# One matmul operand of 512 columns for both parts of the tokens in the first tiles of u, with the selection cut into smaller steps

## The chip, the cores and the metric

The kernel runs on one core of one Trainium2 chip. The metric is the device time of the whole program in microseconds, the median of several runs.

## What is computed

A trunk of two layers over 256 tokens of width 1024. Each layer has a mixer (Mamba-2 SSD in the first, retention in the second), a PEER expert network and a gated per-layer input. The change lies in the expert network, which is dense here: every expert's inner product with every token is computed, and a sparse gate picks from them.

```python
def peer_ffn(h, w_q, sub_keys, u, v):
    q = (xt @ w_q).reshape(T, PEER_HEADS, 2, PEER_HALF)
    sc = jnp.einsum('thcd,hckd->thck', q, sub_keys)
    s1, i1 = lax.top_k(sc[:, :, 0], K)
    s2, i2 = lax.top_k(sc[:, :, 1], K)
    cand = (s1[..., :, None] + s2[..., None, :]).reshape(T, PEER_HEADS, K * K)
    cand_idx = (i1[..., :, None] * NK + i2[..., None, :]).reshape(T, PEER_HEADS, K * K)
    top_s, top_pos = lax.top_k(cand, K)
    idx = jnp.take_along_axis(cand_idx, top_pos, axis=-1)
    gate = jax.nn.softmax(top_s, axis=-1)
    ...
        hid = jax.nn.gelu(jnp.einsum('tkd,td->tk', u[ib], xb), approximate=False)
        return jnp.einsum('tk,tkd->td', (gb * hid), v[ib])
```

There are 256 tokens (T), 8 heads, 128 keys, 16 picks per head (K) and 16384 experts; u and v are 16384 x 1024 in float32.

## The kernel before

Products in float32 are made from numbers split into a high and a low part in fp32r: wh and wl of a weight tile, xh and xl of the tokens. A product is wh xh + wh xl + wl xh.

The function `peer` has, in each layer, a u stage of 128 tiles (128 experts each) and a v stage of 128 tiles. For a u tile, `u_maker` issues four loads of 128 KB on SP and, as soon as they have landed, a transpose of 32 x 32 blocks on DVE (L514); then ACT casts the tile to wh (L519) and POOL subtracts to wl (L522). `get` (called once per tile) starts the cast and the subtraction of the next tile and the load and transpose of the tile after that. Tiles up to 55 are loaded into four places of the arena (`UEND`); from tile 56 on loads and transposes share the four buffers `raw`. wh and wl have two buffers each. The sum of a tile gathers in one of two PSUM banks named `m`: 16 matmuls of 256 columns with wh, alternating xh and xl (L1241, L1242), then 8 with wl (L1245). ACT takes the Gelu from there into H (L1205), one tile later.

Beside these tiles DVE works on the selection: the top 16 of both halves' scores (`sel_codes`), sums of pairs (`sel_sums`), their top 16 (`sel_cand`), positions (`sel_pos`), the softmax (`sel_gate`, whose Exp is on ACT, `sel_sum`, `sel_split`, `sel_ratio`) and the look-up of the picked keys (`sel_idx`: compare, multiply and add over 1024 elements). These steps stand in a list `bg` with a cost each. After a tile's `get`, `pump(1700)` takes steps from the list until the credit is used up. The list ends with `sel_tr`, which transposes the results on TensorE (L1107).

When the list is empty, the gates follow: `g_slot` runs once per tile and moves 64 batches of four tokens through one-hot rows on DVE (`g_hot`), scaling on ACT (`g_lo`), eight small matmuls into a bank `g` (`g_mm`, L1185) and the product with H (`g_apply`, L1199 on DVE). Then the v stage multiplies H, split by `wsplit` (L1256), with v: 12 matmuls of 512 columns per tile (L1279).

All engines run their instructions in the order in which the code records them, in one queue for each engine; waits between engines are semaphores. In the names below arena is the big buffer (H, scores and all of the selection), raw the load buffers, ps the accumulators' banks.

Of the kernel before, what the change touches and what calls it, by code (L numbers as in the profile page):

```python
# [8 lines left out]
F32 = mybir.dt.float32  # L9
# [79 lines left out]
def trunk(ctx: ExitStack, tc: tile.TileContext, a, out, dbg=None, stop=None):  # L89
# [862 lines left out]
    def peer(l, st):  # L952
# [14 lines left out]
        e1 = A[:, S0 + 9856:S0 + 10368].bitcast(F16).rearrange("p (a b c) -> p a b c", a=4, b=16)  # L967
# [71 lines left out]
        def sel_cand(tb, h):  # L1039
            u = 128 * tb + 16 * h  # L1040
            top([cand[:, tb, h + i] for i in range(2)], cand2, [ts_[:, tb, h + i] for i in range(2)],
                [pu[:, u + 16 * i:u + 16 * i + 16] for i in range(2)])
# [23 lines left out]
        def sel_idx(tb, h, c, part):  # L1066
            u = slice(128 * tb + 16 * h, 128 * tb + 16 * h + 64)
            if part == 0:
                dve.tensor_tensor(e1, io16.unsqueeze(1).unsqueeze(1).to_broadcast([P, 4, 16, 16]),
                                  pa[:, c, u].rearrange("p (a b) -> p a b", a=4).unsqueeze(3).to_broadcast(  # L1070
                                      [P, 4, 16, 16]), op=OP.is_equal)
            if part == 1:
                s4 = si.rearrange("p (t h c k) -> p t h c k", t=2, h=8, c=2)[:, tb, h:h + 4, c]
                dve.tensor_mul(e1, e1, s4.unsqueeze(2).to_broadcast([P, 4, 16, 16]))
            if part == 2:
                dve.tensor_reduce(sel[:, c, u].rearrange("p (a b) -> p a b", a=4), e1, axis=AX.X, op=OP.add)
# [38 lines left out]
        bg = [(3100, sel_codes, tb, c0 + c) for c0 in (0, 8) for tb in range(2) for c in range(0, 8, 2)]  # L1115
# [6 lines left out]
        for i in range(4):  # L1122
            bg += [(600, sel_ratio, i), idx[8 + i]]
# [343 lines left out]
```

## Time and profile before

| | us |
|---|---|
| median of 3 runs | 2187.97 (2187.0 to 2191.56) |
| profiled execution | 2188.43 |
| its span, first to last instruction | 2186.7 |
| TensorE busy | 2125.1 (97%) |
| DVE busy | 1577.8 (72%) |
| ACT busy | 1208.1 (55%) |
| POOL busy | 828.5 (38%) |

Busy shares are means over stages with different limits. Within a u stage the start times of TensorE's tiles tell the pace; a wait that ends last shows as idle time before an instruction, with its releaser. The u stage of the first layer runs from 312.3 to 722.4 us after the span's start, that of the second from 1373.9 to 1786.3.

### The profile page before, as it was taken

How to read it: one execution, taken by the hardware profiler on the slowest of the kernel's cores; microseconds unless marked ns; L12 is line 12 of the kernel's file. 1: busy time of each engine (PE TensorE's matmuls, PEld its weight loads, DVE VectorE, ACT ScalarE, POOL GpSimd, SP SyncE). 2: the span in 40 equal slices, each digit the busy share in tenths (PEclk: the TensorE clock that was granted, in tenths of full speed). 3: DMA queues.
4: the chain of work that ended last, by engine and by line, in shares of the span. 5: the costliest groups of instructions: out<-in, count | busy, mean ns of one | idle time of the engine just before them, and what ended most of it. 6: DMA issues, size and time to landing. Idle time of an engine off the chain costs nothing. (4 is left out here: it accounts for less than half of the span.)

```text
span 2186.7 us, 39792 instructions
## 1 busy us (share of the span) xinstructions
PE 2125.1 (97%) x15013; PEld 1967.9 (90%) x15013; DVE 1577.8 (72%) x2641; ACT 1208.1 (55%) x2077; POOL 828.5 (38%) x384
## 2 busy tenths in 40 slices
PE   8988999999999999999999999999999999999997
PEld 8978899999999888888898999999999998888886
DVE  7777578888999655555687466989799985555556
ACT  5654444547888544444554444545588874444444
POOL 3243268877777100000033223888777740000001
PEclk9999999999999999999999999999999999999999
DMA  5423477645555666556556456765555555555553
GB/s 185 145 78 97 161 198 194 184 133 165 155 156 154 188 195 194 193 193 193 188 179 187 128 169 182 192 184 152 153 150 158 155 170 193 195 194 194 194 189 107
DMA packets 219577, 370.27 MB, mean 169 GB/s; under 512 B 24240, under 2 KB 163192, under 8 KB 219384
## 3 DMA queue, kind: packets, MB, share of 16 engines
q1 hardware_dynamic: 219064, 367.19, 56.5%
q8 instruction: 118, 1.93, 0.4%
q14 instruction: 75, 0.61, 0.1%
q10 hardware_dynamic: 320, 0.53, 0.1%
HBM read 364.48 MB, written 1.05 MB: 167 GB/s over the span
## 5 line engine op out<-in xcount | busy, mean ns | idle before, releaser
L139 DVE TENSOR_TENSOR wl<-raw,wh 128x1024 fp32r<-128x1024 f32 x379 | 468.0, 1238 | 402.0 <-ACT wh L136 401.7
L136 ACT CAST wh<-raw 128x1024 fp32r<-128x1024 f32 x429 | 450.6, 1052 | 501.0 <-PE ps L1279 359.0
L522 POOL TENSOR_TENSOR wl<-raw,wh 128x1024 fp32r<-128x1024 f32 x256 | 618.5, 2417 | 200.8 <-ACT wh L519 192.1
L1241 PE MATMUL m<-X,wh 128*128 128x256 f32 x2048 | 514.0, 289 | 0.6 <-ACT arena L1205 0.5
L1279 PE MATMUL ps<-wh,X 128*128 128x512 f32 x2048 | 507.3, 389 | 1.9 <-ACT X L1256 1.9
L1242 PE MATMUL m<-X,wh 128*128 128x256 f32 x2048 | 502.9, 283 | 0.0
L1279 PEld LDWEIGHTS ps<-wh,X 128*128 128x128 f32 x2048 | 384.1, 188 | 82.0 <-ACT X L1256 2.3
L519 ACT CAST wh<-raw 128x1024 fp32r<-128x1024 f32 x256 | 269.0, 1051 | 264.7 <-issue 150.1
L1241 PEld LDWEIGHTS m<-X,wh 128*128 128x128 f32 x2048 | 392.7, 192 | 1.2 <-ACT arena L1205 1.0
L1242 PEld LDWEIGHTS m<-X,wh 128*128 128x128 f32 x2048 | 393.6, 192 | 0.0
L199 PE MATMUL ps<-X,wh 128*128 128x256 f32 x2368 | 331.6, 290 | 12.4 <-ACT wh L136 8.0
L341 POOL TENSOR_TENSOR arena<-arena 128x512 f32<-128x512 f32 x15 | 22.6, 1504 | 815.8 <-ACT arena L339 807.8
L199 PEld LDWEIGHTS ps<-X,wh 128*128 128x128 f32 x2368 | 304.8, 196 | 18.3 <-ACT wh L136 10.2
L1245 PE MATMUL m<-X,wl 128*128 128x256 f32 x2048 | 288.0, 283 | 0.1
L1279 PE MATMUL ps<-wl,X 128*128 128x512 f32 x1024 | 274.7, 389 | 0.0
L1245 PEld LDWEIGHTS m<-X,wl 128*128 128x128 f32 x2048 | 264.8, 192 | 1.1 <-POOL wl L522 1.1
L1279 PEld LDWEIGHTS ps<-wl,X 128*128 128x128 f32 x1024 | 192.2, 188 | 40.0
L514 DVE STREAM_TRANSPOSE raw<-raw 128x1024 f32<-128x1024 f32 x144 | 179.0, 1243 | 39.8 <-DMA raw<-in_peer_u 33.2
L139 POOL TENSOR_TENSOR wl<-raw,wh 128x1024 fp32r<-128x1024 f32 x50 | 124.7, 2500 | 180.3 <-ACT wh L136 149.2
L199 PE MATMUL ps<-X,wl 128*128 128x256 f32 x1184 | 177.3, 287 | 14.2 <-DVE wl L139 10.3
L199 PEld LDWEIGHTS ps<-X,wl 128*128 128x128 f32 x1184 | 157.5, 194 | 17.5 <-DVE wl L139 12.2
L1179 ACT ACTIVATE ol<-ol,G 128x128 f16<-128x128 f16 x512 | 162.8, 398 | 0.1
(263 smaller groups left out, 2015.5 us busy)
## 6 DMA issues: line engine op xcount, KB each, us to landing
raw<-in_peer_v SPq DMA_DIRECT2D x256, 512.0 KB, 4.3
raw<-in_peer_u SPq DMA_DIRECT2D x576, 128.0 KB, 3.0
arena<-in_peer_u SPq DMA_DIRECT2D x448, 128.0 KB, 3.3
raw<-in_ret_w_in SPq DMA_DIRECT2D x48, 512.0 KB, 3.9
raw<-in_ssd_w_in SPq DMA_DIRECT2D x41, 512.0 KB, 3.8
raw<-in_peer_w_q SPq DMA_DIRECT2D x32, 512.0 KB, 4.7
raw<-in_ssd_w_out SPq DMA_DIRECT2D x16, 512.0 KB, 3.8
raw<-in_ple_gate SPq DMA_DIRECT2D x16, 512.0 KB, 4.3
```

The source lines that it names most:

```text
L136: act.copy(wh[:, :n], r[:, :n])
L139: (eng or dve).tensor_sub(wl[:, :n], r[:, :n], wh[:, :n].bitcast(F32))
L199: pe.matmul(self.t[n // 2][:, n % 2], w[:, n * P:(n + 1) * P], x, start=st, stop=sp_, skip_group_check=True)
L341: pool.tensor_add(self.sq[:, 0], self.sq[:, 0], self.sq[:, b])
L514: dve.transpose(t.rearrange("p (k b i) -> p b k i", k=8, b=4), r.rearrange("p (b k i) -> p b k i", k=8, b=4))
L519: act.copy(wh, t)
L522: pool.tensor_sub(wl, t, wh.bitcast(F32))
L1179: act.activation(hl[:, 1, j], hl[:, 0, j], AF.Copy, scale=G1[:, t:t + 1])
L1241: pe.matmul(last, wh[:, s], xh, start=k == 0, stop=False)
L1242: pe.matmul(last, wh[:, s], xl, start=False, stop=False)
L1245: pe.matmul(last, wl[:, s], xh, start=False, stop=k == KD - 1)
L1279: pe.matmul(sums[b], h[:, tb * P:(tb + 1) * P], w[:, n * 512:(n + 1) * 512], start=i == 0 and p == 0, stop=i == P - 1 and p == 2)
```

## The change

While selection steps remain, a u tile is wide: xh and xl of a chunk, which lie in one buffer, are given as one moving operand of 512 columns, so the bank's first half gathers wh xh (+ wl xh) and its second half wh xl. ACT copies the second half into H, DVE adds the first half to it, and ACT takes the Gelu in place one tile later. Copy and add are recorded ahead of the next tile's `get`. The selection's steps are cut: each `top` step is one of its five parts. `sel_idx` is made new: for each of 16 ranks one operation compares and multiplies at once into 16-bit numbers, and `sel_add` adds over the ranks. The list is 107400 credits long instead of 114900.

```diff
-        def sel_idx(tb, h, c, part):
-            u = slice(128 * tb + 16 * h, 128 * tb + 16 * h + 64)
-            if part == 0:
-                dve.tensor_tensor(e1, io16.unsqueeze(1).unsqueeze(1).to_broadcast([P, 4, 16, 16]),
...
-            if part == 2:
-                dve.tensor_reduce(sel[:, c, u].rearrange("p (a b) -> p a b", a=4), e1, axis=AX.X, op=OP.add)
+        def sel_idx(c, r0):
+            v = pa[:, c].rearrange("p (h k) -> p h k", k=16)
+            for r in range(r0, r0 + 4):
+                k = slice(r if c else r // 8 * 8, 16)
+                n = 16 - k.start
+                s1 = si.rearrange("p (h c k) -> p h c k", c=2, k=16)[:, :, c, r:r + 1]
+                dve.scalar_tensor_tensor(e1[:, r, :, k], v[:, :, k], float(r), s1.to_broadcast([P, 16, n]),
+                                         op0=OP.is_equal, op1=OP.mult)
+
+        def sel_add(c, i):
+            dve.tensor_reduce(sel[:, c].rearrange("p (h k) -> p h k", k=16)[:, :, 8 * i:8 * i + 8],
+                              e1[:, :8 * i + 8, :, 8 * i:8 * i + 8].rearrange("p r h k -> p h k r"), axis=AX.X, op=OP.add)
...
-        bg = [(3100, sel_codes, tb, c0 + c) for c0 in (0, 8) for tb in range(2) for c in range(0, 8, 2)]
+        bg = [(620, sel_codes, tb, c0 + c, i) for c0 in (0, 8) for tb in range(2) for c in range(0, 8, 2)
+              for i in range(5)]
         for tb in range(2):
             bg += [(1800, sel_sums, tb)]
-            bg += [(2500, sel_cand, tb, h) for h in range(0, 8, 2)]
+            bg += [(500, sel_cand, tb, h, i) for h in range(0, 8, 2) for i in range(5)]
...
-        idx = [(1200, sel_idx, tb, h, c, k) for tb in range(2) for h in (0, 4) for c in range(2) for k in range(3)]
+        idx = []
+        for c, cost in ((0, (1900, 1900, 1200, 1200)), (1, (1900, 1500, 1000, 700))):
+            idx += [(n, sel_idx, c, 4 * i) for i, n in enumerate(cost)] + [(1800, sel_add, c, 0), (3200, sel_add, c, 1)]
...
             if k in (4, 6):
+                both = X[:, xn[0] % 3]
                 xh, xl = split_x(xm[:, 2 * k - 8:2 * k - 4])
-                xp.extend((xh[:, i], xl[:, i]) for i in range(4))
+                xp.extend((xh[:, i], xl[:, i], both[:, :, i]) for i in range(4))
...
-        last, since = None, 0
+        last, since, wide, late = None, 0, False, None
         for i in range(P):
+            if late is not None:
+                act.activation(H[:, late], H[:, late], AF.Gelu)
+                late = None
+            if wide:
+                act.copy(H[:, i - 1], last[:, T:])
+                dve.tensor_add(H[:, i - 1], last[:, :T], H[:, i - 1])
+                late = i - 1
             wh, wl = get()
             if last is not None:
-                g_slot(i, gelu(i - 1, last))
+                g_slot(i, gelu(i - 1, last) if not wide else lambda: None)
...
+            wide = bool(bg)
+            for k, (xh, xl, xx) in enumerate(xp):
                 s = slice(k * P, (k + 1) * P)
-                pe.matmul(last, wh[:, s], xh, start=k == 0, stop=False)
-                pe.matmul(last, wh[:, s], xl, start=False, stop=False)
-            for k, (xh, xl) in enumerate(xp):
+                if wide:
+                    pe.matmul(last, wh[:, s], xx, start=k == 0, stop=k == KD - 1, skip_group_check=True)
...
+            for k, (xh, xl, xx) in enumerate(xp):
                 s = slice(k * P, (k + 1) * P)
-                pe.matmul(last, wl[:, s], xh, start=False, stop=k == KD - 1)
+                pe.matmul(last[:, :T], wl[:, s], xh, start=False, stop=k == KD - 1, skip_group_check=wide)
```

In the built program 56 tiles of each layer are wide (tiles 0 to 55). SP's and POOL's instructions keep their order. What moves on ACT and DVE shows at three places.

ACT at the start of the u stage, the kernel before: the cast for tile 1, two copies of scores (L1001), the cast for tile 2, the first Gelu (L1205) with its table load, and the next copies.

```order
L519 CAST wh<-raw 128x1024 [waits DVE_49,PE_49,Pool_49] x2
L1001 COPY arena<-g 128x512 [waits PE_49] x2
L519 CAST wh<-raw 128x1024 [waits DVE_49,Pool_49]
L1205 ACT_TABLE_LOAD
L1205 ACTIVATE arena<-m 128x256
L1001 COPY arena<-g 128x512 [waits PE_49] x2
L519 CAST wh<-raw 128x1024 [waits DVE_49,Pool_49]
```

The same place now; L1239 is the copy of a tile's second half, L1236 the Gelu in place.

```order
L519 CAST wh<-raw 128x1024 [waits DVE_49,PE_49,Pool_49] x2
L1001 COPY arena<-g 128x512 [waits PE_49] x2
L1239 COPY arena<-m 128x256
L519 CAST wh<-raw 128x1024 [waits DVE_49,Pool_49]
L1001 COPY arena<-g 128x512 [waits PE_49] x2
L1236 ACT_TABLE_LOAD
L1236 ACTIVATE arena<-arena 128x256 [waits DVE_49]
L1239 COPY arena<-m 128x256
L519 CAST wh<-raw 128x1024 [waits DVE_49,Pool_49]
```

The table load and the first Gelu stood ahead of the second pair of score copies and stand behind it now, and a copy stands ahead of each cast.

ACT around the Exp of the softmax (L1084 of the kernel before), before:

```order
L1205 ACTIVATE arena<-m 128x256 [waits PE_49]
L519 CAST wh<-raw 128x1024 [waits DVE_49,PE_49,Pool_49]
L1205 ACTIVATE arena<-m 128x256 [waits PE_49]
L1084 ACT_TABLE_LOAD
L1084 ACTIVATE arena<-arena 128x256 [waits DVE_49]
L519 CAST wh<-raw 128x1024 [waits PE_49,Pool_49]
L1205 ACT_TABLE_LOAD
L1205 ACTIVATE arena<-m 128x256 [waits PE_49]
```

The same place now (L1086 is the Exp):

```order
L1239 COPY arena<-m 128x256 [waits PE_49]
L519 CAST wh<-raw 128x1024 [waits DVE_49,Pool_49]
L1086 ACT_TABLE_LOAD
L1086 ACTIVATE arena<-arena 128x256 [waits DVE_49]
L1236 ACT_TABLE_LOAD
L1236 ACTIVATE arena<-arena 128x256
L1239 COPY arena<-m 128x256 [waits PE_49]
L519 CAST wh<-raw 128x1024 [waits Pool_49]
```

The cast after the Exp stood directly behind it; now the second table load, a Gelu and a copy stand between them. Each copy waits for TensorE, and the cast behind it no longer does.

DVE in the middle of the codes, before: whole pairs of five steps between transposes.

```order
L1009 MAX arena<-arena 128x8 x2
L1011 MAX_INDEX arena<-arena 128x8 [waits DVE_49] x2
L1014 MATCH_REPLACE arena<-arena 128x128 x2
L1009 MAX arena<-arena 128x8 [waits DVE_49] x2
L1011 MAX_INDEX arena<-arena 128x8 [waits DVE_49] x2
L514 STREAM_TRANSPOSE raw<-arena 128x4x8x32 [waits DMAHW2_49,DMAHW1_49,DMAHW7_49,DMAHW0_49,Pool_49]
L514 STREAM_TRANSPOSE raw<-arena 128x4x8x32 [waits DMAHW5_49,DMAHW4_49,DMAHW6_49,DMAHW3_49,Pool_49]
```

The same place now, with the add of a tile's halves at L1240:

```order
L1240 TENSOR_TENSOR arena<-m,arena 128x256 [waits Activation_49]
L514 STREAM_TRANSPOSE raw<-arena 128x4x8x32 [waits DMAHW5_49,DMAHW4_49,DMAHW6_49,DMAHW3_49,Pool_49]
L1012 MAX_INDEX arena<-arena 128x8 [waits DVE_49] x2
L1010 MAX arena<-arena 128x8 x2
L1240 TENSOR_TENSOR arena<-m,arena 128x256 [waits Activation_49]
L514 STREAM_TRANSPOSE raw<-arena 128x4x8x32 [waits DMAHW2_49,DMAHW1_49,DMAHW7_49,DMAHW0_49,Pool_49]
```

Each iteration now holds one add, one transpose and two or three steps of a pair; the add waits for ACT alone.

## Rows read from the trace of the kernel before

**Rows 1.** Busy time by stage: from:to, length, busy per engine (instructions), clock, DMA.

```profile
345.00:403.00 58.00, 58.00 (x486) 58.00 (x485) 48.65 (x208) 26.95 (x42) 48.51 (x21) 1.00 0.71 187
403.00:460.00 57.00, 57.00 (x478) 57.00 (x477) 54.01 (x112) 29.14 (x42) 47.90 (x20) 1.00 0.65 171
730.00:1060.00 330.00, 330.00 (x1457) 273.25 (x1457) 182.85 (x152) 156.21 (x151) 0.00 (x0) 1.00 0.61 193
```

**Rows 2.** Timeline of TensorE, two u tiles' wl parts: start, length, instruction.

```profile
358.11 1.12 PE L1245 MATMUL m<-X,wl 128*128 128x256 f32 x8
...
360.99 1.12 PE L1245 MATMUL m<-X,wl 128*128 128x256 f32 x8
```

**Rows 3.** Timeline of ACT around the Exp of the first layer.

```profile
423.06 1.28 ACT L1084 ACT_TABLE_LOAD   x1
424.36 0.42 ACT L1084 ACTIVATE arena<-arena 128x256 f32<-128x256 f32 x1
...
425.73 1.28 ACT L1205 ACT_TABLE_LOAD   x1
427.03 0.39 ACT L1205 ACTIVATE arena<-m 128x256 f32<-128x256 f32 x1
```

**Rows 4.** Timeline of ACT at the start of the first u stage.

```profile
318.73 1.28 ACT L1205 ACT_TABLE_LOAD   x1
...
321.83 0.59 ACT L1001 COPY arena<-g 128x512 f32<-128x512 f32 x1 [0.31 <-PE g L999]
322.32 1.05 ACT L519 CAST wh<-raw 128x1024 fp32r<-128x1024 f32 x1
```

**Rows 5.** Timeline of DVE, positions, softmax and adds.

```profile
414.93 0.67 DVE L1048 CAST ps<-arena 128x512 f32<-128x512 uint32 x1
...
417.34 1.24 DVE L514 STREAM_TRANSPOSE raw<-arena 128x1024 f32<-128x1024 f32 x1
418.50 0.16 DVE L1082 COPY ps<-arena 128x16 f32<-128x16 f32 x1
...
420.69 0.40 DVE L1054 TENSOR_SCALAR ps<-arena 128x256 f32<-128x256 f32 x1
...
423.77 1.24 DVE L514 STREAM_TRANSPOSE raw<-arena 128x1024 f32<-128x1024 f32 x1
...
430.63 1.22 DVE L1076 TENSOR_REDUCE arena<-arena 128x64 f32<-128x1024 f16 x1
...
433.35 0.18 DVE L1089 TENSOR_SCALAR ps<-ps 128x16 f32<-128x16 f32 x1
```

**Rows 6.** Timeline of DVE, one pair of codes and the transpose behind it.

```profile
340.05 0.45 DVE L1009 MAX8 arena<-arena 128x8 f32<-128x128 f32 x2
...
342.36 1.23 DVE L514 STREAM_TRANSPOSE raw<-arena 128x1024 f32<-128x1024 f32 x1
343.51 0.45 DVE L1009 MAX8 arena<-arena 128x8 f32<-128x128 f32 x2
```

**Rows 7.** Timeline of TensorE, first matmul of tile 2.

```profile
321.55 0.36 PE L1241 MATMUL m<-X,wh 128*128 128x256 f32 x1
```

**Rows 8.** Timeline of TensorE: tiles 56 and 72 of both layers, the gap between.

```profile
479.07 1.12 PE L1245 MATMUL m<-X,wl 128*128 128x256 f32 x8
...
533.75 1.12 PE L1245 MATMUL m<-X,wl 128*128 128x256 f32 x8
...
1540.61 1.12 PE L1245 MATMUL m<-X,wl 128*128 128x256 f32 x8
...
1573.50 0.64 PE L1185 MATMUL g<-ol,oh 128*128 128x128 f16 x8 [2.64 <-DVE arena L1199]
1576.84 1.72 PE L1245 MATMUL m<-X,wl 128*128 128x256 f32 x8
...
1597.87 1.12 PE L1245 MATMUL m<-X,wl 128*128 128x256 f32 x8
```

**Rows 9.** Timeline of TensorE, first matmuls of the v stage.

```profile
723.33 2.12 PE L1279 MATMUL ps<-wh,X 128*128 128x512 f32 x8 [0.97 <-ACT X L1256]
```

More of the change, by code (lines that the diff above doesn't have):

```diff
@@ L966, in peer @@
         tq = view(S0 + 9344, 256)
-        e1 = A[:, S0 + 9856:S0 + 10368].bitcast(F16).rearrange("p (a b c) -> p a b c", a=4, b=16)
+        e1 = A[:, S0:S0 + 2048].bitcast(F16).rearrange("p (r h k) -> p r h k", r=16, h=16)
         sel = view(S0 + 10880, 4, 256)
@@ L1037, in sel_sums, with sel_cand @@
                         dve.tensor_add(dst[:, :, i * nj:(i + 1) * nj], v1[:, :, i:i + 1].to_broadcast([P, 8, nj]), v2)
-        def sel_cand(tb, h):
+        def sel_cand(tb, h, part):
             u = 128 * tb + 16 * h
             top([cand[:, tb, h + i] for i in range(2)], cand2, [ts_[:, tb, h + i] for i in range(2)],
-                [pu[:, u + 16 * i:u + 16 * i + 16] for i in range(2)])
+                [pu[:, u + 16 * i:u + 16 * i + 16] for i in range(2)], part)
         def sel_pos(part):
@@ L1153, in peer @@
         i4 = bank[0][:, :256].bitcast(F16).rearrange("p (a b) -> p a b", b=4)
-        io16, sm = bank[0][:, 256:272], bank[0][:, 272:288]
+        sm = bank[0][:, 272:288]
         sv2 = bank[0][:, 384:512].rearrange("p (a b) -> p a b", a=8)
@@ L1196, in g_apply @@
             if i:
-                for r in ((slice(0, 4), slice(4, P)) if 4 * b + 4 == T else (slice(0, i),)):
+                for r in ((slice(0, 4), slice(4, i)) if 4 * b + 4 == T else (slice(0, i),)):
                     dve.scalar_tensor_tensor(hv[:, r], pv[:, r], 1.0 / GS, hv[:, r], op0=OP.mult, op1=OP.mult)
@@ L1202, in gelu @@
         def gelu(i, ps):
-            st = stored[0]
+            ps, st = ps[:, :T], stored[0]
             if st < T:
@@ L1237, in peer @@
                         g_slot(i)
-            last = mis.tile([P, 512], F32, name="m")[:, :T]
-            for k, (xh, xl) in enumerate(xp):
+            last = mis.tile([P, 512], F32, name="m")
+            wide = bool(bg)
+            for k, (xh, xl, xx) in enumerate(xp):
                 s = slice(k * P, (k + 1) * P)
-                pe.matmul(last, wh[:, s], xh, start=k == 0, stop=False)
-                pe.matmul(last, wh[:, s], xl, start=False, stop=False)
-            for k, (xh, xl) in enumerate(xp):
+                if wide:
+                    pe.matmul(last, wh[:, s], xx, start=k == 0, stop=k == KD - 1, skip_group_check=True)
+                else:
+                    pe.matmul(last[:, :T], wh[:, s], xh, start=k == 0, stop=False)
+                    pe.matmul(last[:, :T], wh[:, s], xl, start=False, stop=False)
+            for k, (xh, xl, xx) in enumerate(xp):
                 s = slice(k * P, (k + 1) * P)
-                pe.matmul(last, wl[:, s], xh, start=False, stop=k == KD - 1)
+                pe.matmul(last[:, :T], wl[:, s], xh, start=False, stop=k == KD - 1, skip_group_check=wide)
             if i < 2:
```

33 lines of the change are left out of this document (13 added, 20 removed).

## The prediction

> **What bounds the kernel now.** I read first the busy time by stage, then the start times of single tiles, then the waits. In the stretch where u's tiles run beside the selection, TensorE is busy all the time: 58.00 of 58.00 us and 57.00 of 57.00, while DVE has 48.65 and then 54.01, ACT about half and POOL 2.4 us per tile [rows 1]. Two neighbouring tiles reach the same place 2.88 us apart [rows 2]; a tile is 24 matmuls of 256 columns, so one takes 0.120. Nothing else ends last there: the stage is TensorE's, and DVE has 0.2 to 0.5 us to spare per tile. In the v stage 1457 matmuls of 512 columns fill 330.00 us without a gap [rows 1], 0.227 each. The page shares hide a second thing, the hand-over from selection to gates, which I come to below.
>
> **TensorE's saving.** A wide tile has 8 matmuls of 512 columns and 8 of 256: 8 x 0.227 + 8 x 0.120 = 2.776 instead of 2.88, so 0.104 less. The built program has 112 such tiles, 0 to 55 of each of the two u stages: 112 x 0.104 = **-11.65 us**. That is all that the operand can bring. The moving operand is now two runs of 256 floats; no row shows one, so its bounds are 0.227 (the v row) and 0.240 (two old ones, saving nothing). I take 0.227, because two runs of a kilobyte each are nearest to the v stage's one run of two.
>
> **What a wide tile adds.** On ACT a copy and a Gelu of 256 instead of one Gelu, some 0.38 each [rows 3]; with the cast of 1.05 [rows 4] that is 1.8 of 2.776, but in a fixed order. On DVE the add of 256, 0.40 long as other operations of 256 [rows 5], of which some 0.35 counts, since neighbours overlap by 0.08 (the transpose of 1.23 gives way after 1.15 [rows 6]). SP's and POOL's instructions keep their order, so no load and no wl subtraction is moved past another. The copy waits for the whole tile (the add behind it has no wait of its own on TensorE, so the copy's wait covers the last matmul), and the cast of the weights for tile i+1 stands behind the copy of tile i-1. Before, that cast ran when the wh part of tile i-1 had ended; now it runs after its end. In steady state it ends 1.6 after tile i starts (0.16 of the last matmul [rows 2], a signal, 0.38, 1.05), POOL ends at 4.05, and wl is needed at 2.776 + 1.82 = 4.59. So the chain is hidden, with 0.5 us left where it had some 2. Three places use that up, once per u stage.
>
> **The start.** In before the table load for Gelu stands behind the cast for tile 2, in the shadow of the scores [rows 4]. Now the first Gelu comes after the second pair of score copies, and load 1.28, Gelu 0.3 and copy 0.3 stand between these and the cast for tile 3. The copies end at 322.1 (0.3 earlier than 322.42 [rows 4]), the cast would run from 323.95 to 325.0, and tile 2, which started at 321.55 [rows 7] and now at 321.2, ends at 324.0: 1.05 of wait for wh and 0.65 for wl, 1.7 per stage. **+3.4 us** (bounds 2.4 and 4).
>
> **The softmax's Exp.** Load, Exp, load, Gelu took 423.06 to 427.42 on ACT [rows 3]; TensorE did not feel it, since ACT had 1.5 us free per tile. In the new order cast, load, Exp, load, Gelu, copy, cast stand in one row. The Exp waits for DVE, which in that iteration has the add 0.35, a transpose 1.15 [rows 6], and two steps of the gate, 0.6; and it comes late by the step before, position part 0, 2.41 [rows 5], a lag of some 1.9. So the Exp ends 5.3 us after tile 37 starts, the load at 6.6, Gelu and copy at 7.2, the cast at 8.25, while wh was needed at 5.9: 2.4 of wait, 0.65 for wl behind it, 0.35 from the lag itself. 3.4 per stage, **+6.8 us** (bounds: 1.5 per stage without a lag, 4 with a bigger one).
>
> **DVE's lag.** Before, DVE depended on TensorE only through free buffers and could run ahead. Now each add ties it to the tile just ended: it can begin 0.67 after tile i starts, and tile i+1 needs its bank, so a lag of 1.6 us is free and what exceeds it stops TensorE. Per tile DVE has 0.35 + 1.15 + the selection step in 2.776, so 1.27 for selection. A pair of codes takes 2.31 [rows 6] for 5 steps of 620 credits; 1700 credits per tile are 2.74 steps, 1.27: balanced, a lag that wanders under 1. Candidates are lighter. The last 18 tiles are heavy: position parts 1 and 2 fall into one iteration, 3.08 [rows 5], 1.8 too much, of which 0.65 remains after the Exp's stall let DVE catch up; four products of 256 take 1.4; the adds of 1024 cost 1.14 (the old one of 1024 elements [rows 5]) and those of 2048 twice that, 2.2, a tile of 3.7. Carried from tile to tile the lag passes 1.6 at the parts 1 and 2 (0.65), before the first long add (0.2), at it (0.9) and at the second (0.9), and once at the sums of candidates (0.15): 2.8 per stage, **+5.6 us**. The products write 16-bit and read a broadcast from PSUM, a form the trace lacks; bounds 0.34 (net) and 0.44 (seven dependent operations in 3.08 [rows 5]) for each of 256. The term lies between 1 and 10 us.
>
> **The hand-over.** From tile 56 to tile 72 the wl part moved by 54.68 us in the first stage and 57.26 in the second [rows 8]. Eight tiles at 2.88 and eight at 3.41 (2.88 plus the gate's matmuls) are 50.3, so 4.4 and 7.0 are lost: from tile 56 the loads go through the four raw buffers and DVE's transposes wait for them, and the first gate's product comes late, a gap of 2.64 on TensorE in the second stage [rows 8]. Now selection ends at tile 55 where the loads change over, so both fall together, and tiles of 3.41 with useful gate matmuls run where loads held up tiles of 2.88. The first gates still wait for DVE, whose transposes wait for loads. I estimate 4.8 per stage from the two stages' 4.4 and 7.0, nearer to the first, since the second holds the gap of 2.64 and slower matmuls after it: 9.6 against 11.4, **-1.8 us** (bounds -5 and +4).
>
> **The end of u.** The last gate is now applied at tile 123 instead of beyond 127, so the split of H that v waits for, 0.97 in each stage [rows 9], is long done: **-1.9 us**. The v stage itself does not change.
>
> **Sum.** -11.65 + 3.4 + 6.8 + 5.6 - 1.8 - 1.9 = +0.45. The profiled execution took 2188.43 (span 2186.7 and 1.7 around it), 0.46 above the median of 2187.97; on the median 2188.4. The saving is real and is given back, on ACT's order and DVE's queue.
>
> **The rivals.**
> 1. *The chains hold.* If DVE's steps run some 4% shorter than I take them, no lag builds up: its term falls to 0.5 and the Exp's to 3. Sum -8.5, 2179.5. For it: DVE had 9 us free in 58 [rows 1], and the lag is a small difference of large numbers. Against it: 0.35 of add takes most of that.
> 2. *The long adds are slower than one element per cycle.* They read 16-bit numbers 512 bytes apart. At twice the price each stage's four adds (6144 elements) cost 6.4 more, nearly all beyond a lag already at its limit: +12, 2200. It decides from about 1.5 us for 1024 elements; under that the tiles behind, without selection, absorb it. Against it: a copy of 16 numbers 64 bytes apart took 0.16, and an operation on 16 neighbours 0.18 [rows 5]. The Trainium skill, Advanced Engine Details and Errata, Memory Cachelines, speaks for it: accesses to SBUF that each touch another line of 16 bytes pay a penalty. By that rule this rival would be the forecast; the short copy does not show the penalty.
> 3. *TensorE's clock falls in the Exp's gap.* The granted clock is 1.00 in these stretches [rows 1], the level of 2.4 GHz. After the gap of 2.64 us the next wl part took 1.72 instead of 1.12 [rows 8], so part of it ran at 1.2 GHz. A gap of 2.4 and one of 0.65 soon after it could do the same: some 1.7 more in each stage, and with products at 0.44 another 2 to 3: 2194.
> 4. *It doesn't do what it says.* The two runs cost 0.240: no saving, 2200.
>
> **How the numbers follow.** I give the forecast (within 2184 to 2192) 0.44, rival 1 0.30, rival 2 0.09, rival 3 0.14, rival 4 0.03. About 0.2%, 4.4 us, is what a measurement here can tell from no change. Rival 1 alone is faster: 0.30; the others slower: 0.26; same 0.44. The range runs from 2176, rival 1 with a third of its remaining stalls gone too, to 2197, beyond rival 3. It leaves out rivals 2 and 4 and some 0.06 of rival 1's lower end: 0.18.
>
> **What would show it.** In the profile after: wide tiles 2.78 apart in mid-stage (2.88 means rival 4); a TensorE gap near 2.4 behind the Exp whose releaser is ACT's cast, and one of about 1 before tile 3; the add on DVE as releaser of TensorE in the last 18 tiles, with fewer and shorter gaps for rival 1; an add of 2048 at 2.2 us, not 4; v's first matmul without its 0.97. I am wrong if the cast does not stand behind the copy's end, or if the hand-over gets much longer or shorter than 4.8.

## The result, and the profile after

The changed kernel takes 2198.52 us (median of 6, 2196.73 to 2203.10) against 2188.07 (2187.00 to 2191.56): 1.0051 times as long, 95% interval 1.0038 to 1.0065. It is slower by half a per cent, 10.45 us. The forecast was 2188.4 with a range up to 2197. Rival 2, the long adds, at 2200 and with a chance of 0.09, comes nearest; rival 4 has the same 2200, but its sign, tiles 2.88 apart, is not there.

The profiled execution took 2202.94, 4.4 over its median and 14.5 over the profiled one of before. From the first matmul of tile 0 to v's first, its two u stages last 416.33 and 416.09 us; before, 411.02 and 413.45: 7.9 more. Of the rest, 5.1 stand ahead of the first u stage, most of it at one place that the change leaves alone: one operation on DVE took 2.82 instead of 0.68, TensorE waited 4.19 instead of 0.51, and its clock was at half for longer (6.83 instead of 3.41). I count this as chance: a subtraction on POOL began 0.13 ahead of that operation in this execution and 0.73 behind its end in the one of before, and over all profiles of this document the first u stage starts anywhere from 308.8 (e_f32) to 317.5 (e_pieces). Another 1.4 lie between the two u stages. What makes the 10.45 of the medians more than the 7.9 of the stages I did not settle.

Busy time by stage, answering [rows 1], with the same columns:

```profile
345.00:403.00 58.00, 58.00 (x332) 50.97 (x332) 57.02 (x231) 34.59 (x63) 49.95 (x22) 1.00 0.75 189
403.00:460.00 57.00, 54.15 (x305) 46.61 (x304) 53.34 (x172) 34.56 (x59) 45.21 (x19) 1.00 0.65 169
460.00:492.00 32.00, 27.67 (x144) 23.73 (x143) 27.88 (x46) 14.36 (x28) 21.54 (x9) 0.89 0.44 120
```

The columns are TensorE's matmuls, its weight loads, DVE, ACT and POOL. TensorE has gaps now from 403 on, and in the last stretch the granted clock is 0.89, where it was 1.00. DVE, the third busy time, is busy for 57.02 of 58.00 where it was for 48.65: it is the second full engine.

TensorE's timeline: two wide tiles in a row, answering [rows 2], then the first pair of long adds:

```profile
452.37 2.00 PE L1257 MATMUL m<-X,wh 128*128 128x512 f32 x8
454.21 1.12 PE L1263 MATMUL m<-X,wl 128*128 128x256 f32 x8
455.16 2.00 PE L1257 MATMUL m<-X,wh 128*128 128x512 f32 x8
...
459.92 1.11 PE L1263 MATMUL m<-X,wl 128*128 128x256 f32 x8
463.13 3.37 PE L1257 MATMUL m<-X,wh 128*128 128x512 f32 x8 [2.11 <-DVE arena L1240]
466.30 1.42 PE L1263 MATMUL m<-X,wl 128*128 128x256 f32 x8
467.56 1.99 PE L1257 MATMUL m<-X,wh 128*128 128x512 f32 x8
```

Undisturbed, tiles stand 2.79 apart (455.16 - 452.37). Then TensorE waits 2.11 for L1240, the add that frees the bank, and its next eight wide matmuls take 3.17 to the next start (466.30 - 463.13) instead of 1.84 (454.21 - 452.37): it runs at half clock, 1.2 GHz, right behind the gap. The profile shows such a stretch at both pairs of adds in both layers and at no other place of these stages.

DVE's timeline over the same adds:

```profile
455.50 2.01 DVE L1077 TENSOR_REDUCE arena<-arena 128x128 f32<-128x1024 f16 x1
457.43 0.41 DVE L1240 TENSOR_TENSOR arena<-m,arena 128x256 f32<-128x256 f32 x1
457.76 1.23 DVE L514 STREAM_TRANSPOSE raw<-arena 128x1024 f32<-128x1024 f32 x1
458.92 3.74 DVE L1077 TENSOR_REDUCE arena<-arena 128x128 f32<-128x2048 f16 x1
462.58 0.41 DVE L1240 TENSOR_TENSOR arena<-m,arena 128x256 f32<-128x256 f32 x1
```

The adds take 2.01 and 3.74, where the old one of 1024 elements took 1.22 [rows 5]. The sum at 462.58 stands behind the second, and TensorE starts 0.14 after its end.

The start of u on ACT behind the last copy of scores, answering [rows 4], and TensorE there:

```profile
327.38 1.28 ACT L1236 ACT_TABLE_LOAD   x1
328.67 0.42 ACT L1236 ACTIVATE arena<-arena 128x256 f32<-128x256 f32 x1
329.00 0.35 ACT L1239 COPY arena<-m 128x256 f32<-128x256 f32 x1
329.25 1.05 ACT L519 CAST wh<-raw 128x1024 fp32r<-128x1024 f32 x1
```

```profile
330.35 2.11 PE L1257 MATMUL m<-X,wh 128*128 128x512 f32 x8 [0.80 <-ACT wh L519]
332.83 1.22 PE L1263 MATMUL m<-X,wl 128*128 128x256 f32 x8 [0.37 <-POOL wl L522]
```

The Exp on ACT, answering [rows 3], and TensorE behind it:

```profile
427.61 1.28 ACT L1086 ACT_TABLE_LOAD   x1
430.67 0.42 ACT L1086 ACTIVATE arena<-arena 128x256 f32<-128x256 f32 x1 [1.78 <-DVE arena L1085]
431.10 1.28 ACT L1236 ACT_TABLE_LOAD   x1
432.39 0.42 ACT L1236 ACTIVATE arena<-arena 128x256 f32<-128x256 f32 x1
432.71 0.35 ACT L1239 COPY arena<-m 128x256 f32<-128x256 f32 x1
432.96 1.05 ACT L519 CAST wh<-raw 128x1024 fp32r<-128x1024 f32 x1
```

```profile
434.06 2.11 PE L1257 MATMUL m<-X,wh 128*128 128x512 f32 x8 [1.93 <-ACT wh L519]
436.54 1.22 PE L1263 MATMUL m<-X,wl 128*128 128x256 f32 x8 [0.36 <-POOL wl L522]
```

Both go as the prediction told them: load, Gelu and copy stand ahead of the cast, the Exp waits for DVE (1.78), and TensorE waits for the cast and then for wl.

The wl parts of tiles 56 and 72 in both layers, answering [rows 8], and v's first matmuls, answering [rows 9]:

```profile
494.09 1.12 PE L1263 MATMUL m<-X,wl 128*128 128x256 f32 x8
548.05 1.12 PE L1263 MATMUL m<-X,wl 128*128 128x256 f32 x8
...
1562.31 1.12 PE L1263 MATMUL m<-X,wl 128*128 128x256 f32 x8
1616.04 1.12 PE L1263 MATMUL m<-X,wl 128*128 128x256 f32 x8
...
733.75 2.00 PE L1297 MATMUL ps<-wh,X 128*128 128x512 f32 x8
```

Tile 56 to 72 takes 53.96 and 53.73. Fourteen of these sixteen tiles carry gate matmuls now, so 14 x 3.41 + 2 x 2.88 = 53.5 is their bare work, what they take with no wait, and 0.5 and 0.2 are lost. The gap ahead of v is gone.

Distances in the first u stage of the changed kernel, each from the start of a tile's wh part on TensorE to that of the next tile (the second stage is within 0.02 of each; tiles 4 to 53 that are left out stand 2.78 or 2.79 apart; that of tile 55 holds 0.74 of transposes behind the selection):

```
tile   2    3  ...  37   38   39   40   41 ...  46   47   48 ...  53   54   55   56
us   3.84 3.55     3.03 4.96 4.17 2.85 2.89    2.83 5.15 4.42    3.05 5.15 5.18 2.95
```

### The profile page after: what moved, and what is told of

Its sections match the earlier page's. It is cut to its first block, busy times and chain, and to the rows that moved or that the text cites. A ratio compares the mean times of both kernels' runs of the same rounds, so it can differ in the third digit from the quotient of the medians.

```text
span 2201.2 us, 38362 instructions
## 1 busy us (share of the span) xinstructions
PE 2125.9 (97%) x14117; PEld 1927.0 (88%) x14117; DVE 1597.7 (73%) x2785; ACT 1247.9 (57%) x2191; POOL 828.3 (38%) x384
## 5 line engine op out<-in xcount | busy, mean ns | idle before, releaser
L1259 PE MATMUL m<-X,wh 128*128 128x256 f32 x1152 | 292.7, 292 | 0.0
L1263 PEld LDWEIGHTS m<-X,wl 128*128 128x128 f32 x2048 | 272.6, 193 | 12.5 <-POOL wl L522 3.7
L1260 PE MATMUL m<-X,wh 128*128 128x256 f32 x1152 | 282.2, 283 | 0.0
L1257 PE MATMUL m<-X,wh 128*128 128x512 f32 x896 | 230.7, 400 | 15.3 <-DVE arena L1240 9.5
L1260 PEld LDWEIGHTS m<-X,wh 128*128 128x128 f32 x1152 | 220.9, 192 | 0.0
L1259 PEld LDWEIGHTS m<-X,wh 128*128 128x128 f32 x1152 | 220.4, 191 | 0.0
L1257 PEld LDWEIGHTS m<-X,wh 128*128 128x128 f32 x896 | 163.5, 192 | 47.7 <-issue 11.5
L199 PE MATMUL ps<-X,wl 128*128 128x256 f32 x1184 | 177.9, 287 | 14.3 <-DVE wl L139 10.3
```

The lines of the kernel that those rows point to most:

```text
L199: pe.matmul(self.t[n // 2][:, n % 2], w[:, n * P:(n + 1) * P], x, start=st, stop=sp_, skip_group_check=True)
L1257: pe.matmul(last, wh[:, s], xx, start=k == 0, stop=k == KD - 1, skip_group_check=True)
L1259: pe.matmul(last[:, :T], wh[:, s], xh, start=k == 0, stop=False)
L1260: pe.matmul(last[:, :T], wh[:, s], xl, start=False, stop=False)
L1263: pe.matmul(last[:, :T], wl[:, s], xh, start=False, stop=k == KD - 1, skip_group_check=wide)
```

## The experiments

All are compared with the kernel before on the same chip, each with the median of before that was taken beside it. The u stages are those of the one profiled execution, both together, against 824.5 before. e_micro, which only measures operations, ran once and has no row.

| kernel | what differs | u stages | median, against before | ratio (95%) |
|---|---|---|---|---|
| changed kernel | | +7.9 | +10.4 | 1.0051 (1.0038 to 1.0065) |
| e_narrow | new selection, old tiles | -9.0 | -9.3 | 0.9967 (0.9952 to 0.9982) |
| e_wide_old | old selection, wide tiles | +10.3 | +9.9 | 1.0056 (1.0035 to 1.0077) |
| e_late | e_narrow, selection ends 8 tiles later | +8.0 | +10.7 | 1.0047 (1.0030 to 1.0063) |
| e_price | adds read neighbours | -2.2 | -3.3 | 0.9987 (0.9977 to 0.9997) |
| e_pieces | adds in short steps | -3.9 | -2.4 | 0.9991 (0.9981 to 1.0002) |
| e_spread | adds charged more | +9.5 | +10.3 | 1.0053 (1.0036 to 1.0071) |
| e_contig | products scattered, adds read neighbours | +25.1 | +28.7 | 1.0133 (1.0116 to 1.0150) |
| e_tree | 16-bit halves | +4.9 | +6.8 | 1.0037 (1.0024 to 1.0050) |
| e_f32 | 32-bit halves | +7.8 | +9.4 | 1.0047 (1.0031 to 1.0064) |
| e_cast | cast ahead of the copy | +0.3 | +2.8 | 1.0011 (1.0000 to 1.0021) |
| e_best0 | cast, Exp, 16-bit halves | -4.0 | -3.2 | 0.9988 (0.9969 to 1.0008) |
| e_best1 | cast, Exp, 32-bit halves | -5.5 | -5.3 | 0.9976 (0.9964 to 0.9987) |
| e_best2 | cast, Exp, short steps | -15.1 | -15.2 | 0.9929 (0.9911 to 0.9946) |
| e_mix | cast, wide tiles to 33 only | -14.6 | -17.4 | 0.9937 (0.9920 to 0.9955) |

The medians follow the u stages within 4 us, so I read causes from the stages.

**The two halves of the change apart.** e_narrow keeps the new selection and takes the wide tiles away:

```diff
-            wide = bool(bg)
+            wide = False
```

> The new selection with the old tiles of 24 matmuls of 256 columns. Theory (the change's hand-over gains because selection now ends where the loads change over, whatever the tiles are): tiles of 2.88 with no loss at the start, the Exp or the long adds, since nothing there ties TensorE to DVE; hand-over loses 1 us instead of 4.4 and 7.0 and v's wait of 0.97 is gone, 4.5 to 7 per u stage less than before: 2176 to 2179. Rival (the hand-over gained because wide tiles let DVE lag or catch up): hand-over as before, 2186 to 2188.

It came as the theory had it: the median is 2177.79, and the stages are 3.6 and 5.4 shorter, a little less than expected. DVE's long adds are as long here, and TensorE's timeline shows no wait over them:

```profile
463.29 2.03 DVE L1077 TENSOR_REDUCE arena<-arena 128x128 f32<-128x1024 f16 x1
466.39 3.92 DVE L1077 TENSOR_REDUCE arena<-arena 128x128 f32<-128x2048 f16 x1
```

All of its tiles from 3 to 54 are 2.88 apart. So the long adds cost time only where a sum on DVE frees TensorE's bank. The new selection alone wins 9 us, and the wide tiles, which were to save 11.65, lose 17 beside it (7.9 + 9.0).

e_wide_old is the other half: the wide tiles and their sums with the functions and the list of the old selection.

```diff
-        bg = [(620, sel_codes, tb, c0 + c, i) for c0 in (0, 8) for tb in range(2) for c in range(0, 8, 2)
-              for i in range(5)]
+        bg = [(3100, sel_codes, tb, c0 + c) for c0 in (0, 8) for tb in range(2) for c in range(0, 8, 2)]
...
```

> The old selection in its coarse steps with the wide tiles and the new order of sums. Theory: wide tiles 2.79 apart to about tile 63 save 0.087 each, 11 in all; start 3.6 and Exp near 7.6 stay; no long adds (their largest is 1.22 for 1024 elements), so no gap there; the hand-over and the 0.97 ahead of v as before: 2186 to 2190. Rival (coarse steps of 2.3 us pass the 1.6 of lag that is free): gaps behind DVE's add all through the codes, 2195 or more.

My expectation fell, the rival holds in part: the coarse codes cost only 0.8 per stage (tiles 12 to 26), but between tiles 42 and 62 TensorE waits for the sums again and again and loses some 7.5 per stage. Two of the eight waits on TensorE there in the first layer:

```profile
448.40 2.09 PE L1252 MATMUL m<-X,wh 128*128 128x512 f32 x8 [0.72 <-DVE arena L1235]
...
486.44 2.08 PE L1252 MATMUL m<-X,wh 128*128 128x512 f32 x8 [0.80 <-DVE arena L1235]
```

No instruction of the selection is over 1.25 us here. In the kernel before DVE had 3 us free in the 57 from 403 to 460, some twenty tiles [rows 1], and twenty sums of 0.35 want 7. So wide tiles lose beside either selection.

**The price of the long adds.** e_micro adds steps that only measure, on e1's bytes:

```diff
+        bg += [(1700, micro, n) for n in range(9)]
```

> The changed kernel with nine more steps behind the selection, one memset and eight reduces whose results nobody reads, to price them: 64 sums of 16 numbers each, 16-bit, the 16 numbers 2, 16, 32, 128 and 512 bytes apart; 128 sums at 512 bytes; 64 sums of 32-bit numbers 512 bytes apart; 128 sums of neighbours. Theory (stride): 1.2 us at 2 bytes, 2.0 at 512, with a step in between; 32-bit at 512 bytes about as dear as 16-bit; 128 sums twice 64. Rival (the number of results sets it): all of 64 sums alike.

DVE's timeline, in the order 2, 16, 32 and 512 bytes (128 took 2.04), 128 sums at 512, 32-bit at 512, 128 sums of neighbours:

```profile
493.64 1.18 DVE L1088 TENSOR_REDUCE arena<-arena 128x64 f32<-128x1024 f16 x1
...
496.22 1.99 DVE L1088 TENSOR_REDUCE arena<-arena 128x64 f32<-128x1024 f16 x1
...
499.62 2.13 DVE L1088 TENSOR_REDUCE arena<-arena 128x64 f32<-128x1024 f16 x1
...
506.57 1.98 DVE L1091 TENSOR_REDUCE arena<-arena 128x64 f32<-128x1024 f16 x1
...
509.95 3.73 DVE L1091 TENSOR_REDUCE arena<-arena 128x128 f32<-128x2048 f16 x1
...
515.07 1.93 DVE L1094 TENSOR_REDUCE arena<-arena 128x64 f32<-128x1024 f32 x1
...
518.39 2.26 DVE L1096 TENSOR_REDUCE arena<-arena 128x128 f32<-128x2048 f16 x1
```

A sum over neighbours costs 1.1 to 1.15 ns per element, and one at 16, 32, 128 or 512 bytes 1.8 to 2.1. The step that I expected between 2 and 512 bytes lies below 16 already; the width of the numbers hardly matters, and the number of results doesn't.

e_price asks what this price does in the changed kernel. Its adds read the wrong numbers, as many of them, side by side:

```diff
+            n = 64 + 64 * i
+            f = A[:, S0:S0 + 2048].bitcast(F16)[:, :16 * n]
...
-                              e1[:, :8 * i + 8, :, 8 * i:8 * i + 8].rearrange("p r h k -> p h k r"), axis=AX.X, op=OP.add)
+                              f.rearrange("p (h k r) -> p h k r", h=16, r=8 * i + 8), axis=AX.X, op=OP.add)
```

> The changed kernel, but the long adds read 1024 and 2048 neighbouring 16-bit numbers instead of the sixteen 512 bytes apart, so their sums are not those that the computation needs; sizes, order, products and all else stay. Theory (rival 2 of the prediction: the price per element is the cause): 1.2 and 2.3 us, 1.7 to 2.4 less per pair, no gap of 2 on TensorE and no half clock there, 7 to 8 us per u stage less: 2182 to 2185. Rival (DVE is full there in any form): gaps of 1 or more stay, and over half of the 8.3: 2190 or above.

DVE's groups between 440 and 495 us:

```profile
L1079 DVE TENSOR_REDUCE arena<-arena 128x128 f32<-128x2048 f16 x2 | 4.5, 2242 | 0.0
L1079 DVE TENSOR_REDUCE arena<-arena 128x128 f32<-128x1024 f16 x2 | 2.4, 1190 | 0.0
```

The adds now have the durations that the forecast took. TensorE's timeline shows no wait over 0.13 and no half clock at either pair; tiles 46 to 55, 8.3 over their bare work in the changed kernel, are 0.6 over it. So the price is what makes those steps too long. The stage gains only 4 to 6, since tiles 60 and 61, in the hand-over, lose 3.9 in the first layer and 1.8 in the second, where they lost 0.5 and 0.3.

**Cures of the adds, four of which failed.** Three brought a cost of their own, and one did not do what it was to do. e_contig lays the products so that a sum reads neighbours:

```diff
-        e1 = A[:, S0:S0 + 2048].bitcast(F16).rearrange("p (r h k) -> p r h k", r=16, h=16)
+        e1 = A[:, S0:S0 + 2048].bitcast(F16).rearrange("p (h k r) -> p r h k", r=16, h=16)
```

> The products lie so that the 16 numbers of one sum are neighbours; instructions, order and sizes stay. Theory (the long adds are dear because they read 16-bit numbers 512 bytes apart): they fall from 2.02 and 3.74 us to 1.2 and 2.3 to 2.4, the price per element of the old add (1.22 for 1024); the lag of a pair of adds is then 2 x (0.34 + 1.15) + 3.6 - 2 x 2.79 = 1.0, under the 1.6 that is free, so both gaps of 2.1 on TensorE and the stretches at half clock behind them go: about 8.3 us per u stage, 2182 in all. Rival (any long instruction on DVE stops TensorE here): the gaps stay near 2, 2196 to 2198. Rival (the reduce costs by its 128 results and not by its layout): still 2.0 and 3.7, 2198.

Groups on DVE in its first u stage:

```profile
L1072 DVE SCALAR_TENSOR_TENSOR arena<-arena,ps 128x256 f16<-128x256 f32 x9 | 10.5, 1425 | 0.0
...
L1077 DVE TENSOR_REDUCE arena<-arena 128x128 f32<-128x2048 f16 x2 | 4.5, 2250 | 0.0
L1077 DVE TENSOR_REDUCE arena<-arena 128x128 f32<-128x1024 f16 x2 | 2.3, 1174 | 0.0
```

The adds fell to 1.17 and 2.25 as expected, and the products, which now write 16-bit numbers 32 bytes apart, rose from 0.40 to 1.43. The gaps moved to the products. The edit moved the cost and did not test the theory.

e_tree replaces the reduces by additions: it adds one half of the products to the other, then one half of what is left to the other, and so on:

```diff
-            dve.tensor_reduce(sel[:, c].rearrange("p (h k) -> p h k", k=16)[:, :, 8 * i:8 * i + 8],
-                              e1[:, :8 * i + 8, :, 8 * i:8 * i + 8].rearrange("p r h k -> p h k r"), axis=AX.X, op=OP.add)
+            if i == 0:
+                dve.tensor_add(e1[:, :8, :, 8:], e1[:, :8, :, 8:], e1[:, 8:, :, 8:])
+                dve.tensor_add(e1[:, :4], e1[:, :4], e1[:, 4:8])
+            else:
+                dve.tensor_add(e1[:, :2], e1[:, :2], e1[:, 2:4])
+                dve.tensor_add(sel[:, c].rearrange("p (h k) -> p h k", k=16), e1[:, 0], e1[:, 1])
```

> The two reduces of each index become four additions of halves, 16-bit with neighbours side by side, in the same two steps at the same credits. Theory: 1.4 us and 0.9 us instead of 2.02 and 3.74 (1024 results of 16 bit took 0.68, 256 took 0.4), no step is over DVE's 1.27 by more than 0.2, no gap at the adds: 8.3 us per u stage less, 2182. Rival (the gaps come from the steps' place in the order, not from DVE's time in them): gaps stay, 2198.

DVE's timeline, and POOL's at the same time:

```profile
451.57 2.75 DVE L1079 TENSOR_TENSOR arena<-arena 128x1024 f16<-128x1024 f16 x1
```

```profile
451.40 2.37 POOL L522 TENSOR_TENSOR wl<-raw,wh 128x1024 fp32r<-128x1024 f32 x1 [0.41 <-ACT wh L519]
```

This second addition began at 451.57, 0.17 behind POOL's subtraction, and ended at 454.3, half a microsecond after POOL did. e_f32 was to avoid this with 32-bit numbers:

```diff
+        e1 = view(S0, 4096).rearrange("p (r h k) -> p r h k", r=16, h=16)
...
-            idx += [(n, sel_idx, c, 4 * i) for i, n in enumerate(cost)] + [(1800, sel_add, c, 0), (3200, sel_add, c, 1)]
+            idx += [(n, sel_idx, c, 4 * i) for i, n in enumerate(cost)] + [(1700, sel_add, c, 0), (1700, sel_add, c, 1), (1600, sel_add, c, 2)]
```

> The changed kernel with one thing changed, the long adds: the products are written as 32-bit numbers, and each index is added up by halves in three steps (1024, 1024, then 512 and 256 results) instead of two reduces of 1024 and 2048. Reads and writes run over neighbours, and no operand is 16-bit, so nothing waits as the 16-bit additions of halves did (2.75 us where POOL was busy). Theory (DVE's lag over the long adds): steps of 1.2, 1.2 and 1.0 us, no gap of 2 and no half clock at the adds, 8 us per u stage less, start and Exp as in the changed kernel: 2181 to 2184. Rival (DVE is so full there that any form stalls): half or more of the loss stays, 2190 or above.

```profile
455.15 2.50 DVE L1083 TENSOR_TENSOR arena<-arena 128x256 f32<-128x256 f32 x1
```

```profile
455.01 2.36 POOL L522 TENSOR_TENSOR wl<-raw,wh 128x1024 fp32r<-128x1024 f32 x1 [0.45 <-ACT wh L519]
```

An addition of 256 takes 2.50 instead of 0.42, until POOL is done. Both inputs lie in SBUF here, in the 16-bit case too. Sums like L1240, with one input in PSUM, take 0.41 beside POOL, and reduces, which have one input, take their own time there too. The Trainium skill, SBUF — State Buffer, section "SBUF: two separate sides", states this: of an operation of DVE with two inputs from SBUF and one of GpSimd that reads SBUF, whichever starts first blocks the other for its whole instruction. The rows agree: POOL, which is GpSimd, had begun 0.14 and 0.17 earlier.

e_spread leaves the adds and changes their charge:

```diff
-            idx += [(n, sel_idx, c, 4 * i) for i, n in enumerate(cost)] + [(1800, sel_add, c, 0), (3200, sel_add, c, 1)]
+            idx += [(n, sel_idx, c, 4 * i) for i, n in enumerate(cost)] + [(2700, sel_add, c, 0), (5000, sel_add, c, 1)]
```

> The changed kernel with only two numbers of the table changed: the long adds are charged 2700 and 5000 credits instead of 1800 and 3200, so an iteration without selection follows each. DVE does the same work. Theory (a lag that two long adds build up in neighbouring iterations): 2.02 + 1.49 - 2.79 = 0.7 is free, 3.74 + 1.49 - 2.79 = 2.4 leaves a gap of 0.8 instead of 2.1, and the clock stays up or falls for less; 8.3 per stage become 2 to 3, with 1 lost by a later hand-over: 2188 to 2190. Rival (the loss is DVE's time as such): nothing won, 2198 or above.

It did not do what I meant. The list runs a step as long as any credit is left and subtracts its charge afterwards, so the first pair still stood in neighbouring iterations with the same gaps (5.17, 4.38). At the second pair one iteration lay between, but there the loads change over, DVE's transpose waited 2.06 for POOL ahead of the second add, and TensorE 3.56. It is inconclusive on the lag: what the second pair costs now lies at the hand-over.

e_pieces cuts the adds into steps that fit:

```diff
+            h = slice(8 * j, 8 * j + 8) if i == 0 else slice(4 * j, 4 * j + 4)
...
+            idx += [(n, sel_idx, c, 4 * i) for i, n in enumerate(cost)] + [(1300, sel_add, c, j // 4, j % 4) for j in (0, 1, 4, 5, 6, 7)]
```

> The changed kernel with each long add cut along the heads into pieces of 512 elements, 2 and 4 of them, each a step of its own at 1300 credits: same layout and price per element, no step over 1.0 us. Theory (a lag from steps that are longer than the 1.3 us an iteration has, charged too low): no gap at the adds, 8 per stage less; selection ends three tiles later, and the hand-over behind it costs 1 to 3 more per stage: 2184 to 2188. Rival (price alone): the same 11.5 us of adds still stop TensorE for 5 or more per stage, 2192 or above.

```profile
L1078 DVE TENSOR_REDUCE arena<-arena 128x32 f32<-128x512 f16 x8 | 8.5, 1059 | 0.0
L1078 DVE TENSOR_REDUCE arena<-arena 128x64 f32<-128x512 f16 x4 | 4.2, 1062 | 0.0
```

12.7 us of adds at the full price, more than before the cut (11.5), and tiles 42 to 55 stand 2.79 or 2.80 apart. One gap of 1.27 is left at tile 57. So the price does its harm through the length of a step that is charged too little: what counts is how far one iteration goes over what DVE has.

**ACT's order.** e_cast moves the cast ahead of the copy and the late Gelu behind the sum:

```diff
+            wh, wl = get()
             if wide:
                 act.copy(H[:, i - 1], last[:, T:])
                 dve.tensor_add(H[:, i - 1], last[:, :T], H[:, i - 1])
-                late = i - 1
-            wh, wl = get()
+            if late is not None:
+                act.activation(H[:, late], H[:, late], AF.Gelu)
+            late = i - 1 if wide else None
```

> Only the order: the cast of the next weights and the transpose stand ahead of the copy and the add, the late Gelu behind them. Theory (the cast waits behind table loads and Gelu at two places): the 1.8 us lost at tiles 2 and 3 fall to 0.2 or less; at the Exp tile 39 waits for its bank (cast 1.05 and copy 0.35 behind the Exp) instead of for its weights, 3.9 lost become about 2.4; the gaps at the long adds stay: 3 to 3.5 per u stage, 2191 to 2193. Rival (the copy behind the cast frees the bank too late): wide tiles are no longer 2.79 apart but 2.85 or more, and the time is 2198 or above.

Tiles 2 and 3 lose 0.1 instead of 1.8, those at the Exp 1.8 instead of 3.8, a little better than expected, and what TensorE waits for has changed:

```profile
429.58 2.11 PE L1256 MATMUL m<-X,wh 128*128 128x512 f32 x8 [1.38 <-DVE arena L1238]
```

Steady tiles stay at 2.79, so the bank is not freed too late. The losses at the adds stay too.

**The hand-over.** e_late is e_narrow with one number changed:

```diff
-        bg += [(2000, wait), (50, sel_tr, 0), (50, sel_tr, 1)]
+        bg += [(15600, wait), (50, sel_tr, 0), (50, sel_tr, 1)]
```

> The new selection with narrow tiles as in e_narrow, and one number changed: the wait ahead of the hand-over is charged 15600 instead of 2000, so that the selection's end and the first gate come eight tiles later, as in the kernel before, while the loads change over at tile 56 as ever. Theory (the hand-over is cheap if both fall together, and tiles with useful gate matmuls run where the loads hold TensorE up): 4 to 7 lost instead of 1 to 2 in each stage, and v waits 0.97 for the split again: 2184 to 2188. Rival (the new selection's shorter steps make the hand-over cheap): 2177 to 2180.

The loss is larger than expected: 8.5 in each stage against e_narrow. DVE waits up to 3.12 for loads between tiles 64 and 69, and the gate's products come late:

```profile
533.12 0.64 PE L1191 MATMUL g<-ol,oh 128*128 128x128 f16 x8 [1.94 <-DVE arena L1205]
...
728.26 2.12 PE L1297 MATMUL ps<-wh,X 128*128 128x512 f32 x8 [0.71 <-ACT X L1274]
```

The last row is v's first matmul, which waits for the split again. So the end of selection at tile 55, beside the change of the loads, is what makes the hand-over cheap with narrow tiles; that it does the same with wide ones I infer from their like size (1.2 and 1.0 lost).

**The cures together.** e_best0, e_best1 and e_best2 take e_cast's order, put the Exp into a step of its own one iteration behind its subtraction, and cure the adds by 16-bit halves, 32-bit halves and short steps:

```diff
+        def sel_exp():
+            act.activation(sel[:, 2], sel[:, 2], AF.Exp)
...
+        bg += [(1900, sel_pos, 0), (700, sel_gate), (1000, sel_exp), (1100, sel_pos, 1), (1500, sel_pos, 2), (800, sel_pos, 3)]
```

> Three cures together: additions of halves instead of the long reduces (credits 1800 and 1200), the cast ahead of the copy, and the Exp in a step of its own, one iteration behind the subtraction it needs, so that ACT doesn't wait for DVE. Theory (the change's saving is sound and its three stalls are of ACT's order and DVE's steps): steady 4.9, hand-over 3 to 5 and end 1 won in each u stage, less than 1 lost at start, Exp and adds: 2167 to 2172. Rival (each cure brings the next wait, of wl or of a bank): 2180 or above.

> Wide tiles with all three stalls treated: cast ahead of the copy and the late Gelu, the Exp in a step of its own, additions of 32-bit halves in three steps. Theory: of the u stage of e_best0 (408.8 in its first layer) the 6 us at the adds go, 403 per stage against 411.0 and 413.5 before and 407.4 and 408.1 with narrow tiles: 2166 to 2171 in all. Rival (wide tiles have DVE so full that the lag comes back elsewhere): no better than narrow tiles, 2176 or above.

> e_best1 with the adds in pieces of 512 elements instead of the 32-bit halves. Theory: 409.5 per stage less 6 at the adds, plus 1 to 3 for a later hand-over: 404 to 406, 2170 to 2175. Rival (the later hand-over costs what the adds gave): 2178 or above, no better than narrow tiles.

The first two missed (2185.32, which can't be told from the kernel before, and 2182.15): the Exp costs 0.3 now, but the halves stall beside POOL (5.00 and 4.91 from tile to tile in e_best0's first stage, 5.33 and 5.08 in e_best1's). e_best2 met its expectation: 404.4 and 404.9 per stage, 2172.59. e_mix instead keeps wide tiles from where DVE is full:

```diff
-            wide = bool(bg)
+            wide = i < 34
```

> The new selection, the cast ahead of the copy, and wide tiles only for tiles 0 to 33, ahead of the Exp and of the steps that fill DVE; narrow tiles from 34. Theory (the wide operand is sound where DVE has room, and all its losses lie behind tile 36): 34 x 0.087 = 3 per stage less than e_narrow's 407.4 and 408.1, 404.5, with no gap at the Exp or the adds: 2171 to 2174. Rival (some cost of the wide tiles sits in the first half too): 2177 or above.

404.9 in both stages, 2170.38 in all, as expected, 0.6% under the kernel before; between e_mix and e_best2 the runs do not decide.

## Why the prediction was wrong

The terms against what the two u stages of the changed kernel show, from distances of tiles:

| term | predicted | measured |
|---|---|---|
| wide tiles | -11.65 | 112 x (2.88 - 2.793) = -9.7 |
| start | +3.4 | 2 x 1.8 = +3.6 |
| Exp | +6.8 | 2 x 3.8 = +7.6 |
| DVE's lag | +5.6 | 2 x (8.3 + 0.2) = +17.0 |
| hand-over | -1.8 | 1.2 + 1.0 - 11.4 = -9.2 |
| end of u | -1.9 | -1.9 |
| sum | +0.45 | +7.4 (the stages: +7.9) |

(The 0.74 of the transposes behind the selection counts with the hand-over, as before. The lag is 8.3 at tiles 46 to 55 and 0.2 at tiles 40 and 41 in each stage.)

**The step that failed is the price of the long adds** in the part on DVE's lag. I took 1.14 and 2.2 from the old add of 1024, a row whose numbers lie side by side, and kept that price for numbers 512 bytes apart. They took 2.02 and 3.74. I had the mechanism (add, bank, TensorE), the limit of the lag and the rival with its bound of 1.5, and gave it 0.09 because a copy of 16 numbers 64 bytes apart took 0.16: at the 0.8 ns per element that the adds lost, 16 elements lose 13 ns, which a row of 0.16 us can't show. I had set the Trainium skill, Advanced Engine Details and Errata, section Memory Cachelines, against that row: accesses to SBUF that each touch another line of 16 bytes pay a penalty. The trace agrees: e_micro's reduce took 1.18 with neighbours and 1.99 at 16 bytes. By that rule the forecast would have been 2200.

That rival 2's 2200 lies so near 2198.52 is partly luck. It takes the adds at 6.4 more per stage (6.7 by the prediction's own 1.14 and 2.2), where they took 4.8 more, and it has neither the half clock (+6.6) nor the short hand-over (-7.4), which nearly cancel. At the price that I took, the lag itself was too large: with adds of 1.19 and 2.24, e_price loses some 0.8 per stage in tiles 40 to 55, where I had 2.8.

**The lag had a second price.** Of the 8.3 lost at the adds per stage some 3.3 are half clock behind the gaps (1.33 in the wh part and 0.31 in the wl part of tile 48, and as much at the second pair). I had this mechanism in rival 3 at the Exp, where the clock stayed at 1.00 in spite of a gap of 1.93; it came at the adds. In other runs it did not stay up there: behind the same wait, 1.93, it fell to half in the first layer of e_contig, and behind 1.94 in that of e_f32. And the lag depends on DVE's whole load: e_wide_old stalls without a long add. Reading that DVE had 3 us free in 57, I should have set 20 sums of 0.35 against it.

**The hand-over** had the right mechanism (both fall together) and a size far too small: I put the new loss near the old ones, where 1.2 and 1.0 are left of 4.4 and 7.0. This is what the prediction named as a sign of being wrong. e_late, which brings the offset between loads and gates back and loses 8.5 by it, points to that offset as the old loss. This error of 7.4 the other way hid two thirds of the 11.4 by which the lag was off.

**The rest held.** Start and Exp came within 0.8, with the waits and releasers named; by the order alone e_cast takes away 1.7 of the 1.8 at the start and 2.0 of the 3.8 at the Exp, and an Exp in a step of its own leaves 0.3 of these (e_best2). The wide matmul costs 0.229 rather than 0.227, 0.017 more a tile, 1.9 in all. The gap ahead of v went. Rival 1, no lag, and rival 4, no saving, are out.

## What to carry to other kernels

Price an operation by a row with the same access pattern (which numbers it reads, and how far apart); a row with as many elements is not enough, and a short row proves nothing about a price per element. Before work is added to an engine that does not set the pace, look at the stretch in which it is fullest and at what newly waits for it there: the same adds cost nothing until a sum behind them held TensorE's bank. A saving on one engine can be taken where the others have room, here the first 34 tiles, and left where they have none.

## What the runs showed of the hardware

- A reduce on DVE costs 1.1 to 1.15 ns per element over neighbours and 1.8 to 2.1 at 16, 32, 128 and 512 bytes, for 16-bit and (at 512) 32-bit numbers alike (e_micro). Scattered writes are dearer still: products with 256 results 32 bytes apart took 1.43 us instead of 0.40 (e_contig).
- An addition on DVE with both inputs in SBUF, begun while POOL subtracts, lasts beyond the end of POOL's instruction: 2.50 us instead of 0.42 for 256 elements (e_f32). A reduce, or an addition with an input in PSUM, doesn't wait (0.41 at L1240).
- TensorE's granted clock fell to half behind a wait of 2.11 at the adds and stayed at 1.00 behind one of 1.93 at the Exp, in both layers of the changed kernel. The length of the wait alone does not decide it: behind 1.93 at the Exp it fell to half in e_contig's first layer (0.50 from 432.3 to 435.7), and behind 2.08 at an add it stayed at 1.00 in e_tree's (454.8 to 458.2).
